# A hybrid mLSTM and pooling layer on eight cores: first-tile loading, engine of the square sums, store times, schedule weights and the place of the final norm changed together

## Chip, cores and metric

The kernel is one layer with an mLSTM (a recurrent layer whose state is a matrix). It runs on all 8 cores of one Trainium2 chip, one sequence per core with no exchange between them. The metric is device microseconds of the slowest core. A program on all cores has two states here: in some executions the cores of one die show a lower granted TensorE clock (down to 0.81 of full, against 0.993 to 0.998), and the time is some per cent longer. Such executions are called slow, whatever the kernel, and are left out of every comparison. Where few executions were fast, I also compare the mean span of single cores on undisturbed dies (all four cores of the die at a clock of 0.992 or more). This "mean core" is below the time of the slowest core but scatters less: for the changed kernel the means of its 20 undisturbed dies lie between 5299.5 and 5306.8 us. The kernel before has mean cores of 5400.3, 5401.0 and 5401.1 us in the calls on three chips, and of 5404.8 in the one profiled execution of the first call. The changed kernel's own call names no chip, so a mean core that differs from it by up to about 4 us is not read as an effect. Where a single step is compared, I also give its mean over the eight cores of each profiled execution, cut at the same count of matmuls on every core (of weight loads, where a trace misses matmul records).

## The reference, cut to what matters

```python
def reference(x, ffn1_..., w_in, b_in, ..., ffn2_..., final_norm_g):      # x (8, 8192, 1024) float32
    x = x + 0.5 * swiglu_ffn(rms_norm(x, ffn1_norm_g), ffn1_w_gu, ffn1_w_down)     # F1, hidden 2816
    x = x + hybrid_mixer(rms_norm(x, mix_norm_g), w_in, ...)                       # the mix
    x = x + 0.5 * swiglu_ffn(rms_norm(x, ffn2_norm_g), ffn2_w_gu, ffn2_w_down)     # F2
    return rms_norm(x, final_norm_g)                                               # final norm
# hybrid_mixer: one projection gives q,k,v,o,u and gates; branch A is an mLSTM over chunks with a norm
# for each head, branch B a trailing mean over 2/4/8/16 tokens; sigmoid gates merge both, one output product
```

## The kernel before

A core takes its sequence in 16 tiles of 512 tokens, kept feature-major (partition, chunk of 128 features, token). A step is a pipeline stage: its main list of units holds F2 of tile i-1 and F1 of tile i+1, its side list the mix of tile i. `interleave` merges both lists into one order by the costs written beside the units. All engines then run that fixed order, each waiting on semaphores for what it reads.

```python
def interleave(main, side, lo, hi):
    ...
            want = lo + (hi - lo) * (ds / tside)      # ds: cost of the side units taken so far
            take_main = dm / tm < want                # dm: cost of the main units taken so far
```

Weights stand in memory as 53 pieces in float32. The first uses of a piece load it with a cast to bf16 (issued by GpSimd); at one use the bf16 copy is stored to scratch, and later uses load that copy (issued by SyncE). A slot that is being stored from is given back one piece later. Six slots hold pieces.

```python
            def store_at(k):                       # at which use of piece k its bf16 copy is stored
                if k < P_F1 + 11:
                    return 0
                if P_QK <= k < P_F2:
                    return k % 2
                return 1
            ...
            def load(tok, s):
                ...
                cast = n <= store_at(k)            # so a late store means one more cast load
```

The norms need a sum of squares over features. ScalarE squares one chunk, GpSimd adds it to the others, and one product with a matrix of ones sums over partitions; then Ln and Exp on ScalarE give the factor.

```python
            def sq(k, x, a):
                ...
                act(sqt[:, k % 2, :], x[:, k, :], AF.Square)
                o = accb[a] if k == KC - 1 else acc[a]
                tt(o[:, :], acc[a][:, :], sqt[:, k % 2, :], ALU.add, eng="pool")

            def norm_rs(a, r, s):
                b = bank(s)                        # main and side have four PSUM banks each, in turn
                mm(PS(b), onesb, accb[a][:, :], True, True)
                act(rs[r][:, :], PS(b), AF.Ln, bias=EPS, scale=1.0 / D)
                act(rs[r][:, :], rs[r][:, :], AF.Exp, scale=-0.5)

            def with_final(main, i):               # final norm and output of tile i, inside F1 of a later tile
                add = final_units(i)               # norm_rs, then four times two products and a store
                ...
                for q, p in enumerate(add):
                    main.insert(4 + 2 * q, p)      # after the fourth product of F1's gate and up list
```

In the mix, the head norm of branch A (Ln and Exp over `sm`) is followed by four units that transpose and gate the result, and by the merge products that read it (`ys`).

```python
                for h in range(H):
                    def run(h=h):
                        ...                        # four transposes on TensorE
                        stt(yaT[:, h, :], PSB(b, 0, 512), pcol(HNG + h), sig[:, h, :], ALU.mult, ALU.mult)
                    us.append((0.5, run))          # the scheduling cost
```

The softmax here doesn't subtract the row's maximum and nothing guards it: scores larger than these inputs give would overflow.

## Time and profile before

| | before |
|---|---|
| median of the first 4 runs | 5425.17 us (5409.37 to 6419.6, the highest a slow one) |
| span of the cores, profiled run | 5396.8 to 5413.9 us, clock 0.993 to 0.994 |
| mean core, undisturbed dies of all calls | 5401.1 us (108 cores) |
| TensorE busy | 97 % of the span |
| one steady step (12 of them) | 330.0 us |
| idle time per steady step that the trace lists | 4.13 us |

TensorE has the work, so the profile is read for TensorE's waits. The waits view adds up the gaps over a stretch by what ended them (columns: engine, tile and line that waited, what came last, us in total, times, longest). For the twelve steady steps, 1096 to 5056 us, of the kernel before:

```profile
PE ps L349 <- DVE ys L377: 23.2, 12, 1.9
PE ps L349 <- ACT tF L370: 12.0, 12, 1.0
PE ps L349 <- POOL accb L373: 8.6, 12, 0.7
PE ps L349 <- DVE hid L373: 5.8, 12, 0.5
```

`ps` is a PSUM bank, to which products write their sums; `xnF` and `xnM` are the normed inputs of the two feed-forward parts and of the mix, `hid` the hidden features, `tF` the result of a Silu, `ys` branch A's result and `accb` the sum of squares. Each gap is small and comes exactly 12 times: 49.6 us in all. The same view of 230 to 1065 us, the early steps, on the slowest core:

```profile
PE ps L349 <- DMA w<-scr: 16.4, 2, 15.1
PE ps L349 <- DMA w<-wsrc: 10.7, 6, 3.0
```

`w<-wsrc` is a cast load, `w<-scr` a load of the stored copy. One row of the page's groups is the exchanges of ScalarE's activation table (columns: line, engine, operation, count, busy us, mean ns, idle before):

```profile
L370 ACT ACT_TABLE_LOAD x221 | 283.5, 1283 | 135.6 <-PE ps L349 113.5
```

### The profile page before, as it was taken

How to read it: one execution, taken by the hardware profiler on the slowest of the kernel's cores; microseconds unless marked ns; L12 is line 12 of the kernel's file. 1: busy time of each engine (PE TensorE's matmuls, PEld its weight loads, DVE VectorE, ACT ScalarE, POOL GpSimd, SP SyncE). 2: the span in 40 equal slices, each digit the busy share in tenths (PEclk: the TensorE clock that was granted, in tenths of full speed). 3: DMA queues.
4: the chain of work that ended last, by engine and by line, in shares of the span. 5: the costliest groups of instructions: out<-in, count | busy, mean ns of one | idle time of the engine just before them, and what ended most of it. 6: DMA issues, size and time to landing. Idle time of an engine off the chain costs nothing.

```text
span 5413.9 us, 74501 instructions; the slowest of 8 cores (5396.8 to 5413.9 us)
## 1 busy us (share of the span) xinstructions
PE 5231.0 (97%) x25247; PEld 2424.5 (45%) x25758; DVE 2074.2 (38%) x3032; ACT 1688.9 (31%) x2973; POOL 1013.1 (19%) x995
## 2 busy tenths in 40 slices
PE   7999989999999999999999999999999999999998
PEld 3444434444444444444444444444444444444443
DVE  2253444244442434434334342443424444343432
ACT  2132333233332323323233232333323333232321
POOL 0121233021121202212022130211212012120310
PEclk9999999999999999999999999999999999999999
DMA  9778799545444344444444444454443444434443
GB/s 221 138 179 173 152 216 237 172 152 179 156 162 166 139 172 159 168 159 143 169 156 170 150 150 170 152 180 152 152 175 137 177 154 173 158 140 159 147 146 121
DMA packets 144130, 883.36 MB, mean 163 GB/s; under 512 B 16144, under 2 KB 18832, under 8 KB 80016
## 3 DMA queue, kind: packets, MB, share of 16 engines
q1 hardware_dynamic: 130368, 800.65, 42.3%
q0 software_dynamic: 12672, 77.08, 9.3%
q8 instruction: 215, 3.52, 0.3%
q14 instruction: 155, 1.27, 0.1%
q10 hardware_dynamic: 720, 0.84, 0.1%
HBM read 873.78 MB, written 81.79 MB: 177 GB/s over the span
## 4 chain that ended last, share of the span: by engine, by line
PE 84%; DVE 5%; ACT 3%; issue 3%; DMA 3%; POOL 1%; DVEq 0%; ACTq 0%; SPq 0%; POOLq 0%
PE ps L349 84%; DVE xnF L377 3%; ACT L370 2%; DMA w<-wsrc 1%; DVE x L377 1%; ACT rs L370 1%; DMA w<-scr 1%; DMA scr<-w 1%; PE ps L353 0%; DVE xnM L377 0%; POOL accb L373 0%; POOL acc L373 0%; ACT sqt L370 0%; ACT tM L370 0%; DVE Cf L373 0%
## 5 line engine op out<-in xcount | busy, mean ns | idle before, releaser
L349 PE MATMUL ps<-xnF,w 128*128 128x512 bf16 x10700 | 2491.8, 380 | 44.3 <-ACT tF L370 13.4
L349 PEld LDWEIGHTS ps<-xnF,w 128*128 128x128 bf16 x10912 | 1063.8, 98 | 1315.9 <-issue 68.0
L349 PE MATMUL ps<-hid,w 128*128 128x512 bf16 x5329 | 1222.2, 380 | 12.5 <-DMA w<-wsrc 5.9
L349 PE MATMUL ps<-xnM,w 128*128 128x512 bf16 x4360 | 1044.8, 380 | 38.1 <-DVE ys L377 24.4
L373 DVE TENSOR_TENSOR hid<-tF,ps 128x512 bf16<-128x512 f32 x682 | 466.5, 686 | 1590.8 <-PE ps L349 1409.0
L373 POOL TENSOR_TENSOR acc<-acc,sqt 128x512 f32<-128x512 f32 x372 | 488.2, 1316 | 2609.3 <-ACT sqt L370 2601.8
L370 ACT ACTIVATE tF<-ps 128x512 f32<-128x512 f32 x704 | 418.6, 597 | 1283.4 <-PE ps L349 1228.9
L349 PEld LDWEIGHTS ps<-hid,w 128*128 128x128 bf16 x5456 | 529.7, 98 | 624.7 <-issue 14.4
L349 PEld LDWEIGHTS ps<-xnM,w 128*128 128x128 bf16 x4448 | 434.7, 98 | 557.7 <-issue 43.9
L377 DVE SCALAR_TENSOR_TENSOR x<-ps,x 128x512 f32<-128x512 f32 x384 | 264.7, 689 | 705.8 <-PE ps L349 658.6
L370 ACT ACTIVATE sqt<-x 128x512 f32<-128x512 f32 x434 | 265.4, 625 | 727.8 <-DVE x L377 577.3
L370 ACT ACTIVATE tM<-ps,pvh 128x512 f32<-128x512 f32 x320 | 219.8, 687 | 785.6 <-PE ps L349 778.8
L377 DVE SCALAR_TENSOR_TENSOR tM<-zy,pv_s,tM 128x512 f32<-128x512 bf16 x384 | 295.2, 771 | 198.1 <-POOL tM L385 159.8
L370 ACT ACT_TABLE_LOAD x221 | 283.5, 1283 | 135.6 <-PE ps L349 113.5
L377 DVE SCALAR_TENSOR_TENSOR tB<-tM,ps 128x512 bf16<-128x512 f32 x256 | 175.8, 687 | 244.6 <-PE ps L349 240.3
L349 PE MATMUL ps<-qkT,w 128*128 128x512 bf16 x1060 | 252.0, 379 | 0.9
L377 DVE SCALAR_TENSOR_TENSOR xnF<-x,pv_s,rs 128x512 bf16<-128x512 f32 x248 | 206.5, 899 | 113.5 <-ACT rs L370 113.4
L385 POOL TENSOR_SCALAR tM<-zy,pv_s 128x512 f32<-128x512 bf16 x128 | 92.9, 729 | 640.4 <-ACT zy L370 585.8
L349 PEld LDWEIGHTS ps<-qkT,w 128*128 128x128 bf16 x1088 | 106.5, 98 | 128.4
L370 ACT ACTIVATE zy<-ps,pv_s 128x512 bf16<-128x512 f32 x128 | 87.5, 684 | 203.0 <-PE ps L349 200.3
L349 PE MATMUL ps<-poolT,w 128*128 128x512 bf16 x530 | 136.6, 379 | 0.7
L349 PE MATMUL ps<-ys,w 128*128 128x512 bf16 x528 | 136.5, 379 | 0.8
(94 smaller groups left out, 2298.8 us busy)
## 6 DMA issues: line engine op xcount, KB each, us to landing
w<-scr SPq DMA_DIRECT2D x409, 1024.0 KB, 5.1
w<-scr SPq DMA_DIRECT2D x224, 704.0 KB, 4.2
w<-scr SPq DMA_DIRECT2D x116, 768.0 KB, 4.4
w<-wsrc POOLq DMA_DIRECT2D x44, 1024.0 KB, 18.2
out<-x SPq DMA_DIRECT2D x64, 512.0 KB, 3.8
x<-x SPq DMA_DIRECT2D x15, 2048.0 KB, 12.2
scr<-w SPq DMA_DIRECT2D x29, 1024.0 KB, 20.0
w<-wsrc POOLq DMA_DIRECT2D x32, 704.0 KB, 15.0
```

Source lines behind the costliest of these rows:

```text
L349: P.op("pe", lambda e: e.matmul(out, lhsT, rhs, start=start, stop=stop), reads=[lhsT, rhs], writes=[out])
L370: P.op("act", lambda e: e.activation(out, in_, func, **kw), reads=rd, writes=wr)
L373: P.op(eng, lambda e: e.tensor_tensor(out, in0, in1, op), reads=[in0, in1], writes=[out])
L377: P.op("dve", lambda e: e.scalar_tensor_tensor(out, in0, scalar, in1, op0, op1), reads=rd, writes=[out])
L385: P.op(eng, lambda e: e.tensor_scalar(out, in0, s1, s2, op0, op1), reads=rd, writes=[out])
```

## The change

The change aims at idle time of TensorE and removes none of its work. It slices the first weight piece and reorders that piece's columns so that a slice serves a whole product; it holds tile 1 back until tile 0 is there; it moves the square additions of steps 0 to 2 and one per step later from GpSimd to VectorE; it stores half of the F1 and F2 down pieces, and half of F2's gate and up pieces, one use later; it stretches the scheduling costs of three mixes by 1.7; it moves the final norm from unit 4 to unit 14; it raises the scheduling cost of the last transposing unit from 0.5 to 1.5; and it gives the last tile a shorter end. It also takes the pooled product first in the merge, lets the mixes of steps 1 and 2 end a little earlier (upper limit 0.92 instead of 0.95), and moves four scalings of a constant (`pb`) in step 0 together. The diff, cut to its core:

```diff
@@ store_at
-                return 1
+                if k < P_QK:
+                    return 1 + k % 2
+                return 1 if k < P_QK or k % 2 else 2
@@ squares
-            def sq(k, x, a):
+            sq_eng = ["dve"]                       # set to "pool" from step 3 on
+            def sq(k, x, a, eng=None):
...
-                tt(o[:, :], acc[a][:, :], sqt[:, k % 2, :], ALU.add, eng="pool")
+                tt(o[:, :], acc[a][:, :], sqt[:, k % 2, :], ALU.add, eng=eng or sq_eng[0])
@@ start
-            load_x(1)
...
-            pieces.prime([0])
+            for q in range(4):
+                c0 = q * 1024
+                dma("pool", P.dma_chan(f"w0_{q}"), wS[0][:, c0:c0 + 1024], wsrc_d[P_F1][:, c0:c0 + 1024], ...)
+            dma("sp", ch_x[1], xb[1][:, :, :], x_d[1], reads=[x0[:, 6:8, :]], writes=[xb[1][:, :, :]])
@@ gate and up products: new column order of a piece
-                        c0 = (256 if up else 0) + jj * 128
+                        c0 = (2 * jj + up) * 1024
@@ down_units: last square of F1 on VectorE; the last tile squares and scales chunk by chunk
+                if sqs == i:
+                    us.append((0.0, lambda: sq(KC - 1, xb[sqs % XB], 0, "dve" if which == "F1" else None)))
+                if last:
+                    us.insert(0, (0.0, lambda: act(sm[:, 11, 0:1], sm[:, 8, 0:1], AF.Ln)))
+                    us.append((0.0, lambda: square_sum(KC - 1)))
@@ mix_units(i, a, lat=1.0): waiting units cost lat times as much; lat is 1.7 in steps 1, 2 and 15
-                @u(6.0)
+                @u(7.0 * lat if i < 3 or lat > 1 else 6.0)
...
-                    us.append((0.5, run))
+                    us.append((0.5 if h < H - 1 else 1.5, run))
...
-                        for wh, src in ((0, yaT), (1, poolT)):
+                        for wh, src in ((1, poolT), (0, yaT)):
@@ with_final
-                    main.insert(4 + 2 * q, p)
+                    main.insert(14 + 2 * q, p)
@@ end
-            for _, p in final_units(nt - 1):
-                p()
+            act(rs[0][:, :], PS(4), AF.Ln, bias=EPS, scale=1.0 / D)
+            act(rs[0][:, :], rs[0][:, :], AF.Exp, scale=-0.5)
+            ...                                    # eight products with rs and four stores
```

## The prediction

> **What bounds the kernel now.** I read the cores view first: all eight span 5396.8 to 5413.9 us at a clock of 0.993 to 0.994, so the profiled run is a fast one. Then the page, for the busiest engine:
>
> ```profile
> span 5413.9 us, 74501 instructions; the slowest of 8 cores (5396.8 to 5413.9 us)
> PE 5231.0 (97%) x25247; PEld 2424.5 (45%) x25758; DVE 2074.2 (38%) x3032; ACT 1688.9 (31%) x2973; POOL 1013.1 (19%) x995
> ```
>
> TensorE has the work, and the change removes none of it. Only its idle time (183 us) and its slow-clock time can go. The windows view, cut at the steps of the program (columns: stretch, length, busy time with counts for PE, PEld, DVE, ACT, POOL, then clock, DMA share, GB/s), shows where these lie:
>
> ```profile
> 24.00:240.00 216.00, 204.96 (x881) 89.88 (x900) 50.58 (x77) 42.54 (x68) 18.37 (x27) 0.98 0.84 172
> 240.00:511.00 271.00, 255.45 (x1236) 117.98 (x1260) 110.45 (x160) 80.43 (x150) 65.07 (x71) 0.97 0.82 179
> 511.00:736.00 225.00, 214.46 (x1060) 99.91 (x1079) 97.63 (x144) 75.76 (x141) 58.12 (x69) 0.98 0.85 165
> 736.00:1096.00 360.00, 331.28 (x1578) 152.26 (x1610) 142.69 (x202) 112.68 (x195) 79.07 (x79) 0.96 0.80 214
> 1096.00:1426.00 330.00, 324.18 (x1578) 150.91 (x1608) 128.45 (x189) 105.84 (x186) 61.03 (x57) 1.00 0.45 160
> 5056.00:5279.00 223.00, 214.56 (x1060) 100.16 (x1078) 90.76 (x137) 75.75 (x141) 45.10 (x44) 0.98 0.40 140
> 5398.00:5414.00 16.00, 0.38 (x1) 0.10 (x1) 6.40 (x9) 3.14 (x4) 1.26 (x1) 0.63 0.32 131
> ```
>
> Step 3 (736 to 1096) holds the same 1578 matmuls as a steady step and takes 360 us, not 330; steady steps (12 of them, 1096 to 5056) hold a full clock. Last, the timeline of TensorE, whose brackets give each gap and what ended it. One steady step has four gaps:
>
> ```profile
> 1430.40 0.38 PE L349 MATMUL ps<-accb,cbf 128*128 128x512 bf16 x1 [0.72 <-POOL accb L373]
> 1589.40 1.89 PE L349 MATMUL ps<-xnF,w 128*128 128x512 bf16 x8 [0.48 <-DVE hid L373]
> 1592.28 5.34 PE L349 MATMUL ps<-xnF,w 128*128 128x512 bf16 x23 [1.00 <-ACT tF L370]
> 1602.17 1.89 PE L349 MATMUL ps<-xnM,w 128*128 128x512 bf16 x7 [1.94 <-DVE ys L377]
> ```
>
> Step 3 has the largest gap of the run, and the end has another:
>
> ```profile
> 817.35 3.57 PE L349 MATMUL ps<-w,xnM 128*128 128x512 bf16 x8 [15.14 <-DMA w<-scr]
> 5401.00 0.38 PE L349 MATMUL ps<-accb,cbf 128*128 128x512 bf16 x1 [3.41 <-POOL accb L373]
> ```
>
> **What the skill says.** (1) "TensorE: Matmul & The Clock Gate", section "Wait — 56ns, not 53.3ns?": matmuls of 512 columns start 215.7 ns apart when warm and 426.7 ns when cold. The trace agrees: 8 take 1.73 us here, and after the 15.14 us gap 8 take 3.57 us. So an idle stretch costs more than its gap. (2) "ScalarE: Activation LUTs", section "What ACT_TABLE_LOAD costs": 1283 ns plus a drain of 1380 ns per switch. The page's row has 1283 ns for one of 221 loads; no such drain shows, for at 1592.15 a load starts 0.01 us after an activation ends and the next starts at 1593.45. (3) "SBUF — State Buffer", section "SBUF: two separate sides": VectorE and GpSimd take one port pair as an exclusive lock for a whole instruction when VectorE has two SBUF inputs. Agreed: eight norm products take 5.39 us with POOL idle and 8.42 us (at 247.76) or 10.44 us (at 731.70) with POOL adding squares. (4) "DMA: Bandwidth & Descriptors", section "Queues, rings and completion order": each DMA engine alternates between queues packet by packet. This fits the start, where x0's third quarter lands at 17.12, just after the first weight piece (its store is issued at 16.93), although quarters one and two landed at 6.8 and 9.2.
>
> **The change, part by part.**
>
> Start. The first weight piece comes in four slices of shorter rows, and x1 waits for x0. x1 stood behind x0 in the same queue, so its delay frees little; what helps is that x0's last two quarters meet shorter weight packets. From 9.2 us, 1 MB of x0 and as much weight at about 250 GB/s take 8 us: x0 complete at some 17 us instead of 19.9. The chain behind it (norm, first matmul at 24.15) is unchanged: 3 us. Risk: weights 2 to 6 are now issued after x1 (near 30 us, before 21.7); the first is needed near 51 us and a 2 MB cast load took about 8 us (5.04 MB bf16 in 40 us), so this is hidden.
>
> Step 0. Four scalings of pb ran just ahead of their matmuls and made two gaps of 1.6 us (85.66, 96.12). They move together to an earlier point: 3 us. They wait for pb, itself now held until weight 2 has landed: about 53 us against 58, so hidden.
>
> Steps 0 to 2: squares move from POOL to VectorE. This frees the port and the POOL queue, which also issues the cast loads (three are issued together at 277.99, behind additions). Step 1 takes 270 us for about 250 of work: 704 main matmuls at 0.216 plus a mix of 98 (the 326 us of a gapless steady step less 228 for 1056 matmuls). Its gaps are norm 0.81 + 1.27, xnM into the gate products 3.5, loads 1.58 + 2.98 + 2.67 + 1.25, and slow clock after them 5: 19. I leave 1.3 for xnM (a chain of 8.5 us behind 33 matmuls of 7.1 us) and 2 for loads: 16 gained. Step 2: norm gaps of 3.5 and the last 0.77 go, 3.3 for xnM, 2 of clock and 1.5 of the mix stay: 5.5 gained.
>
> Step 3. Casting and storing twice overload the DMA. Using 8 us per cast, about 3.5 per 1 MB store or scratch load (5.1 to landing) and 16 for x and out, the first half asks 11 x 11.5 + 5 x 3.5 + 16 = 160 us of 115 us of matmuls. With stores of the even pieces one use later it asks 138, and the buffers had already absorbed about 25 of the old excess of 45. So nearly all of 15.14 + 0.41 + 2.78 goes with 4 us of slow clock; I leave 3. The head (0.26 + 0.98 + 1.29 + 1.08 from the port, 1.40 + 2.31 from three norms exchanging activation tables, 2.5 clock, 1.2 at ys) is some 11 us; 3 stays because eight square additions queue on VectorE. Sum: 22.3 + 11 less 6, call it 26 for rounding and for deferred stores in step 4.
>
> Steady steps. The final norm moves from unit 4 to unit 14. At unit 4 it takes a PSUM bank (the 0.48), meets the head norm's table loads (1258.42, 1260.25, 1262.16) and puts 6.5 us of products before the ys products (the 1.94). Without it the sixth unit takes its bank from a finished product, and only about 0.2 us of the 1.00 stays (silu ready at 1262.15 against 1262.0). Pooled-branch products ahead of ys help too. The last square addition of F1 goes to VectorE, 0.7 instead of 1.27 us, starting earlier: 0.72 becomes about 0.1. Gain 4.13 - 0.3 = 3.8, times 12: 45.5.
>
> Step 15 and end. Cost factors of 1.7 spread the mix: of 2.73 + 0.98 + 0.78 and the clock 4.5 is gained. At the end the last matmul falls at 5397.6 and the end 16.3 later. The new tail is product and square 1.6, matmul 0.5, Ln and Exp 1.3 without a table load, eight products 5, DMA 3.8: 12.3. Seven more sum matmuls cost 1.5: net 2.5.
>
> Sum: 3 + 3 + 16 + 5.5 + 26 + 45.5 + 4.5 + 2.5 = 106 us.
>
> **The rivals.** (a) New waits at the new place: the norm moved to unit 14 meets tanh gates, and its two table switches hold ScalarE for 3.8 us. For it: 221 loads already. Against: four banks for each stream, some 10 us of TensorE work. If it costs 2 us a step, 24 of the 45 vanish: 5340. (b) The DMA stays the bound early: even F2 pieces are cast three times, so step 4 has 6 casts more, and loads queue behind the x load as at 787.18 to 817. For: a DMA share of 0.80 to 0.85 over steps 0 to 3. Against: step 4 asks about 122 us in 115, with full buffers. Cost 10 to 20 us: 5330. (c) Early stages clear entirely, as a change tuned on a chip would: 5 to 10 us more, near 5305. (d) VectorE becomes the bound: 38% busy makes this unlikely.
>
> **Range and chances.** The three fast runs before are 5409, 5415 and 5435, mean 5420. From 106 I take 6 for waits that I can't see, and start from 5418, between this mean and their median: 5318 us. 2% faster needs under about 5311, so the threshold lies inside the error of the step-3 and step-1 terms. Range 5296 to 5344; faster 0.40, within 0.59, slower 0.01.
>
> **What would show it.** Steady steps of 326 us with no gap at ys; step 3 near 334 and step 1 near 254; first weight matmul near 21; last matmul to end near 12. A steady step still at 329 or a load gap above 8 us between 240 and 1400 would make it wrong.

## The result, and the profile after

The changed kernel is correct and takes 5314.74 us (median of 11 runs, 5308.09 to 6310.66). The kernel before took 5415.46 us beside it (median of 17, 5409.37 to 6419.6). The ratio is 0.9821, with a 95 % interval of 0.9795 to 0.9847: 1.8 % faster, with the 2 % line inside the interval. A ratio here is the mean time of one kernel's fast runs over that of the other's in the same rounds, so it is not quite the ratio of these medians. The mean core went from 5401.1 to 5302.6 us (80 cores), 98.5 us less; for the changed kernel the means of its 20 undisturbed dies lie between 5299.5 and 5306.8 us.

The page's first lines of the changed kernel, and its table loads:

```profile
span 5310.7 us, 74865 instructions; the slowest of 8 cores (5293.8 to 5310.7 us)
PE 5241.4 (99%) x25765; PEld 2423.7 (46%) x25765; DVE 2099.5 (40%) x3095; ACT 1659.7 (31%) x2950; POOL 936.1 (18%) x951
L370 ACT ACT_TABLE_LOAD x197 | 252.8, 1283 | 126.5 <-PE ps L349 100.2
```

TensorE is at 99 %, and there are 24 table loads fewer, two for each steady step. (The trace of before misses some 2 % of the matmul records: it has 25247, beside 25758 weight loads. So its PE busy time is not compared.) The windows view, cut at the steps, has the columns of the prediction's windows: stretch, length, busy time with counts for PE, PEld, DVE, ACT, POOL, then clock, DMA share, GB/s. Steps 1, 2 and 3 of the changed kernel:

```profile
234.85:497.47 262.62, 252.73 (x1256) 117.23 (x1255) 121.95 (x188) 80.50 (x150) 39.63 (x54) 0.98 0.82 180
497.47:716.61 219.14, 213.96 (x1079) 99.71 (x1078) 101.60 (x154) 75.71 (x141) 39.79 (x56) 0.99 0.88 175
716.61:1058.99 342.38, 330.44 (x1610) 151.55 (x1609) 141.61 (x206) 112.34 (x196) 69.17 (x72) 0.99 0.73 196
```

Measured from the first matmul of a step to the first of the next, on the profiled (slowest) core of each kernel:

| stretch | before | after | gained | predicted | gained, mean of 8 cores |
|---|---|---|---|---|---|
| start | 24.15 | 21.36 | 2.8 | 3 | 2.6 |
| step 0 | 217.08 | 213.49 | 3.6 | 3 | 3.8 |
| step 1 | 270.14 | 262.62 | 7.5 | 16 | 8.5 |
| step 2 | 224.64 | 219.14 | 5.5 | 5.5 | 6.0 |
| step 3 | 360.07 | 342.38 | 17.7 | 26 | 18.7 |
| 12 steady steps | 3959.9 | 3905.2 | 54.7 | 45.5 | 54.7 |
| step 15 | 222.89 | 214.40 | 8.5 | 4.5 | 7.9 |
| last step and end | 135.07 | 132.13 | 2.9 | 2.5 | 1.4 |
| sum | 5413.9 | 5310.7 | 103.2 | 106 | 103.6 |

The waits of the twelve steady steps of the changed kernel, in the form shown for before:

```profile
PE ps L349 <- DVE accb L373: 0.7, 2, 0.4
```

Three of the four rows are gone and 8.6 us of the fourth have become 0.7. The early steps kept waits for weights, but other ones. First the slowest core, then another core of the same execution, 230 to 1065 us:

```profile
PE ps L349 <- DMA w<-wsrc: 7.4, 1, 7.4
PE ps L349 <- DMA w<-scr: 5.3, 1, 5.3
```

```profile
PE ps L349 <- DMA w<-wsrc: 1.1, 2, 0.8
PE ps L349 <- DMA w<-scr: 0.2, 1, 0.2
```

The program is the same on both; only the transfers fall differently. The eight cores lose 5.6, 12.7, 7.9, 2.0, 8.3, 3.7, 8.0 and 1.3 us in this way, where they lost 14.9 to 27.1 before, and the core with the most is the slowest. The timeline of TensorE (start, length, engine, line, operation, tiles, size, count; in brackets the gap before and what ended it) places its two waits, and one of the gaps left at the head of step 3:

```profile
454.49 1.01 PE L349 MATMUL ps<-qkT,w 128*128 128x512 bf16 x2 [7.37 <-DMA w<-wsrc]
723.66 8.46 PE L349 MATMUL ps<-xnF,w 128*128 128x512 bf16 x32 [1.80 <-DVE x L377]
820.43 1.01 PE L349 MATMUL ps<-xnM,w 128*128 128x512 bf16 x2 [5.26 <-DMA w<-scr]
```

The wait at 454 is new, and all eight cores have it (0.8 to 7.4 us). The product that waits is the first of the mix's output (`qkT`). Its weight piece is cast at its first use in both kernels; what is new are the third cast loads of F1's down pieces, which before were read from scratch by then. With them in the queue, cast loads of 1 MB take 23.6 us to land between 400 and 470 us (median of two on this core), where the kernel before took 13.6 between 405 and 475 (also of two). At the end there is no table load, and the eight products take 6.26 us:

```profile
5299.98 0.60 ACT L370 ACTIVATE rs<-ps 128x512 f32<-128x512 f32 x1 [0.62 <-PE ps L349]
5301.40 6.26 DVE L373 TENSOR_TENSOR x<-x,rs 128x512 f32<-128x512 f32 x8 [2.92 <-ACT rs L370]
```

From the last down product (ended 5297.7) to the end it is 13.0 us, against 16.3 before.

### The profile page after: what moved, and what is told of

Read it like the earlier page. It is cut to its first block, busy times and chain, and to the rows that moved or that the text cites. A ratio compares the mean times of both kernels' runs of the same rounds, so it can differ in the third digit from the quotient of the medians.

```text
span 5310.7 us, 74865 instructions; the slowest of 8 cores (5293.8 to 5310.7 us)
## 1 busy us (share of the span) xinstructions
PE 5241.4 (99%) x25765; PEld 2423.7 (46%) x25765; DVE 2099.5 (40%) x3095; ACT 1659.7 (31%) x2950; POOL 936.1 (18%) x951
## 3 DMA queue, kind: packets, MB, share of 16 engines
q0 software_dynamic: 15120, 89.14, 10.6%
## 4 chain that ended last, share of the span: by engine, by line
PE 94%; DVE 2%; DMA 2%; ACT 1%; issue 1%; POOL 0%; SPq 0%; DVEq 0%; ACTq 0%; POOLq 0%
PE ps L349 93%; DVE tM L377 1%; DMA scr<-w 1%; DVE xnF L377 1%; PE ps L353 1%; DMA w<-wsrc 0%; DMA w<-scr 0%; ACT L370 0%; DVE xnM L377 0%; ACT rs L370 0%; DMA x<-x 0%; DVE x L377 0%; POOL tM L385 0%; DVE x L373 0%; DVE hid L373 0%
## 5 line engine op out<-in xcount | busy, mean ns | idle before, releaser
L349 PE MATMUL ps<-xnF,w 128*128 128x512 bf16 x10912 | 2494.8, 380 | 10.6 <-DVE xnF L377 4.6
L373 POOL TENSOR_TENSOR acc<-acc,sqt 128x512 f32<-128x512 f32 x324 | 424.8, 1315 | 2368.9 <-ACT sqt L370 2296.7
L370 ACT ACT_TABLE_LOAD x197 | 252.8, 1283 | 126.5 <-PE ps L349 100.2
L377 DVE SCALAR_TENSOR_TENSOR xnF<-x,pv_s,rs 128x512 bf16<-128x512 f32 x248 | 184.8, 810 | 99.1 <-ACT rs L370 99.1
L397 POOL DMA_DIRECT2D w<-wsrc x105 | 57.2, 546 | 571.7 <-PE ps L349 442.7
```

The source lines that it names most:

```text
L349: P.op("pe", lambda e: e.matmul(out, lhsT, rhs, start=start, stop=stop), reads=[lhsT, rhs], writes=[out])
L370: P.op("act", lambda e: e.activation(out, in_, func, **kw), reads=rd, writes=wr)
L373: P.op(eng, lambda e: e.tensor_tensor(out, in0, in1, op), reads=[in0, in1], writes=[out])
L377: P.op("dve", lambda e: e.scalar_tensor_tensor(out, in0, scalar, in1, op0, op1), reads=rd, writes=[out])
L397: P.op(eng, lambda e: e.dma_start(out=out, in_=in_), reads=list(reads), writes=list(writes), chan=chan)
```

## The experiments

Twelve kernels ran. All were correct. Most take the changed kernel and undo one part; two put one part alone on the kernel before. Times are of fast runs; "mean core" is as defined above.

| kernel | fast runs, us | mean core (cores) | steady 12 steps |
|---|---|---|---|
| before | 5407.7 to 5435, one 5465.1 | 5401.1 (108) | 3959.9 |
| changed | 5308.1 to 5316.7, one 5365.7 | 5302.6 (80) | 3905.2 |
| 1 norm back at unit 4 | 5310.3, 5310.6, 5312.9 | 5304.5 (32) | not cut |
| 2 norm at 14 alone | 5367.2, 5393.5 | 5359.5 (24) | 3916.7 |
| 3 norm at 4 and old cost | 5361.2 | 5354.1 (12) | 3954.3 |
| 4 new cost alone | 5361.9, 5364.4, 5366.4 | 5354.7 (32) | 3914.7 |
| 5 all stores as before | 5328.0, 5330.2, 5330.6 | 5322.3 (32) | 3905.2 |
| 6 F1 stores as before | 5312.7, 5313.0, 5317.0 | 5306.0 (24) | not cut |
| 7 squares on GpSimd | 5316.0 | 5306.4 (12) | not cut |
| 8 no stretch | 5328.2, 5328.7, 5331.4 | 5320.5 (28) | 3904.6 |
| 9 whole first piece, old end | 5315.3 | 5305.7 (8) | not cut |
| 10 tile 1 not held back | 5309.3 | 5298.8 (12) | not cut |
| 11 attempt | 5307.9 to 5311.8, five | 5302.0 (44) | not cut |
| 12 attempt, fewer deferred | 5307.5, 5308.2 | 5302.6 (32) | not cut |

### 1. The final norm back at unit 4

```diff
-                    main.insert(14 + 2 * q, p)
+                    main.insert(4 + 2 * q, p)
```

> The changed kernel with only the place of the final norm undone (unit 4 again instead of 14). Theory A, the place of the norm is what removed the gaps of 0.48, 1.00 and 1.94 us: each of the 12 steady steps grows from 325.4 to about 328.8 us and the kernel from 5315 to about 5355. Rival B, the 1.94 us went because of the unit of other work after the last transpose and because the pooled products now come first: the steps grow only by 1.5 us (0.48 and 1.00), the kernel to about 5333. Rival C, the gaps went because of something else (squares on VectorE): below 5322.

Measured: 5310.28, 5310.64 and 5312.93 us; ratio to before 0.982 (0.9798 to 0.9842), the same as the changed kernel's. The place of the final norm can be undone at no cost, so undoing it does not bring back the gaps that the prediction put down to it. The timeline of ScalarE near the beginning of an F1 list shows what the prediction missed:

```profile
1212.13 0.52 ACT L370 ACTIVATE sm<-sm 128x16 f32<-128x16 f32 x2 [2.37 <-DVE sm L377]
1213.19 1.28 ACT L370 ACT_TABLE_LOAD   x1
1214.48 1.08 ACT L370 ACTIVATE tF<-ps 128x512 f32<-128x512 f32 x2
1216.19 1.28 ACT L370 ACT_TABLE_LOAD   x1 [0.63 <-PE ps L349]
1217.49 0.60 ACT L370 ACTIVATE rs<-ps 128x512 f32<-128x512 f32 x1
```

The head norm's Ln and Exp (`sm`) run before the first Silu (`tF`) of the list, while the table for Ln and Exp is still in place. In the kernel before they stood behind that Silu and cost a table load on each side. Something else in the change had moved them: a theory for the next runs.

### 2. The final norm at unit 14, alone

```diff
 (kernel before)
-                    main.insert(4 + 2 * q, p)
+                    main.insert(14 + 2 * q, p)
```

> The kernel before with only the place of the final norm changed (14 instead of 4). Theory A: steady steps fall from 330.0 to about 326.6 us (the 0.72 us at the mix norm stays) and the kernel from 5414 to about 5373. Rival B: to 328.5 us and about 5396. Rival C: above 5405. If A holds both here and in the run that undoes it, the place of the norm is worth some 40 of the 103 us on its own.

Measured: one undisturbed run of 5367.23 us, and 5393.45; ratio 0.9948 (0.989 to 1.0005), too few fast runs to say much. The mean core settles it: 5359.5, that is 41.6 us less than before. In the steady steps the waits view has one row left:

```profile
PE ps L349 <- POOL accb L373: 8.6, 12, 0.7
```

(This trace is of the 5393.45 us execution, whose slowest core ran below full clock early on; in these steady steps its clock was 1.00.) So alone, the move does what the prediction said of it. Undone, it costs nothing. Both can be true only if another part does the same. The page still counts all the table loads of the kernel before:

```profile
L370 ACT ACT_TABLE_LOAD x221 | 283.5, 1283 | 135.6 <-PE ps L349 115.3
```

Here the head norm still stands between two Silus, with a load on each side (1279.59 and 1281.42), and only the final norm has gone, to 1306.04. The waits of TensorE vanished without one table load fewer: what counts is which work stands in the queue together, not the number of loads.

### 3. Unit 4 and the old scheduling cost

```diff
-                    us.append((0.5 if h < H - 1 else 1.5, run))
+                    us.append((0.5, run))
...
-                    main.insert(14 + 2 * q, p)
+                    main.insert(4 + 2 * q, p)
```

> The changed kernel with the final norm at unit 4 and the last transpose at its old scheduling weight of 0.5 (the pooled products still first). Undoing the place alone cost nothing, doing it alone gained 3.6 us a step. Theory, the weight of 1.5 shifts the head norm's Ln and Exp ahead of the first Silu, so that either measure suffices: with both undone the gaps come back, the steady step is 328.5 to 329.5 us and the kernel near 5355. Rival, the order of the products is what makes the place harmless: the step stays at 325.5 and the kernel near 5315.

Measured: 5361.16 us; mean core 5354.1, 51.5 us more than the changed kernel. The twelve steps take 3954.3 us, 49.1 more, and the three old rows are back in the waits of this stretch:

```profile
PE ps L349 <- DVE ys L377: 23.6, 12, 2.3
PE ps L349 <- ACT tF L370: 12.0, 12, 1.0
PE ps L349 <- DVE hid L373: 5.8, 12, 0.5
```

ScalarE in one of these steps:

```profile
1876.26 0.60 ACT L370 ACTIVATE tF<-ps 128x512 f32<-128x512 f32 x1
1876.88 1.28 ACT L370 ACT_TABLE_LOAD   x1
1878.17 0.53 ACT L370 ACTIVATE sm<-sm 128x16 f32<-128x16 f32 x2
1878.71 1.28 ACT L370 ACT_TABLE_LOAD   x1
1880.01 0.60 ACT L370 ACTIVATE tF<-ps 128x512 f32<-128x512 f32 x1
1880.62 1.28 ACT L370 ACT_TABLE_LOAD   x1
1881.92 0.60 ACT L370 ACTIVATE rs<-ps 128x512 f32<-128x512 f32 x1
```

Silu, load, head norm, load, Silu, load, final norm: ScalarE exchanges its table for every small piece of work, and in the same stretch TensorE waits 0.48 us (for a bank, by the prediction's reading), 1.00 us for a Silu and 1.9 us for `ys`. Again 221 table loads. Together, runs 1 and 3 show that the place can be undone as long as the cost stays. That each part suffices alone, run 2 shows for the place and run 4 for the cost. The pooled product comes first in this run too, and the wait for `ys` is back in full (23.6 us, 23.2 before): that order alone does not remove it.

### 4. The new scheduling cost, alone

```diff
 (kernel before)
-                    us.append((0.5, run))
+                    us.append((0.5 if h < H - 1 else 1.5, run))
```

> The kernel before with one edit: the scheduling cost of the last of the four transposes-and-gate products of ya is 1.5 instead of 0.5, and the final norm stays at unit 4. If this weight is enough by itself, as the run with the place undone and the run with place and weight undone say together, a steady step takes about 326.4 us, the gap of 1.94 us at the ya products is gone, and the kernel takes about 5370 us (5360 to 5385). Rival: the weight only counts together with the other parts of the change (squares, order of the gate products); then a steady step stays at 329 to 330 us and the kernel at 5400 to 5415 us.

Measured: 5361.89, 5364.40 and 5366.44 us. The ratio of 0.9867 (0.9744 to 0.9989) rests on two fast runs of before, one of them at 5465; the mean core of 5354.7 is 46.4 us below before. The twelve steps take 3914.7 us (326.2 each), with these waits:

```profile
PE ps L349 <- POOL accb L373: 8.6, 12, 0.7
PE ps L349 <- DVE hid L373: 0.6, 1, 0.6
```

One number in a scheduling list, with no instruction added or removed, is worth nearly half of the whole change. How it works can be read from `interleave`: a larger cost at the end of the side list raises its total, so every earlier side unit is taken a little sooner, and the products after the raised unit a little later. By the costs in the list, one unit more moves the order by about 228 x 0.95 / 146 = 1.5 us of main products (an estimate from these costs). That is enough to put the head norm ahead of the first Silu (in this trace `sm` starts at 1247.02, the table load at 1248.08 and the Silu at 1249.37), and the wait for `ys` is gone. Table loads fall to 195. What is left, 0.7 us a step, is the wait for the last square addition on GpSimd, which the change moves to VectorE: 3914.7 - 3905.2 = 9.5 us for twelve steps, of which 8.6 are this wait.

### 5. All stores as before

```diff
-                if k < P_QK:
-                    return 1 + k % 2
-                return 1 if k < P_QK or k % 2 else 2
+                return 1
```

> The changed kernel with the old store times (no piece is cast a third time). Theory, spreading the stores removed the 15 us wait for a scratch load in step 3: that wait comes back at 10 to 15 us on the cores, with waits for cast loads in step 3 of 2 to 4 us; step 3 grows from 342 to about 358 us, the kernel to about 5330. The late wait of 7.4 us near 454 us goes. Rival, what removed it is the POOL queue, freed of squares so that casts are issued in time: step 3 stays within 3 us of 342 and the kernel within 4 us of 5315.

Measured: 5327.99, 5330.17 and 5330.6 us, ratio to before 0.9854 (0.9831 to 0.9876) where the changed kernel has 0.9821; mean core 19.7 us above the changed kernel. Step 3 takes 355.5 us in place of 342.4. The cores wait 16 to 27 us for weights between 230 and 1065 us, as they did before the change. One of them:

```profile
PE ps L349 <- DMA w<-wsrc: 15.3, 7, 2.9
PE ps L349 <- DMA w<-scr: 7.7, 1, 7.7
```

The deferred stores carry about 20 us, and most of it in step 3: 13.1 us on the slowest cores, 17.7 in the mean of eight. This is the prediction's reason, and it holds in the main. The expectation missed the form: not one scratch wait of 10 to 15 us came back (the longest is 7.7), but several waits of up to 2.9 us for cast loads, 15.3 us on this core.

### 6. Only the stores of F1 as before

```diff
-                    return 1 + k % 2
+                    return 1
```

> The changed kernel with the old store times for the F1 down pieces alone (cast twice, stored on the second use); F2 keeps the change. Theory, the third cast of the odd F1 pieces made the new wait near 454 us (1 to 7 us by core), and the old waits of 3 to 9 us near 290 to 315 us come back in its place, as when both halves were undone: the sum of load waits between 230 and 1065 us, 1.3 to 12.7 us by core in the changed kernel, stays within 4 us and so does the time (5315). Rival, the F1 half only adds casts: the wait near 454 goes and nothing comes back, 5306 to 5310. Second rival, the F1 half carries the gain: load waits of 15 us and more, 5325 or above.

Measured: 5312.69, 5313.03 and 5316.99 us. Against the changed kernel's 5314.74 this is no difference, and the mean core's 3.4 us is within the 4 us of scatter. The new wait at 454 is gone, but two others stand in its place:

```profile
286.23 2.53 PE L349 MATMUL ps<-hid,w 128*128 128x512 bf16 x11 [2.03 <-DMA w<-wsrc]
303.62 1.86 PE L349 MATMUL ps<-hid,w 128*128 128x512 bf16 x4 [7.26 <-DMA w<-wsrc]
```

Storing F1's pieces early makes the loads of step 1 late near 286 and 303 us; storing them late makes a load late at 454 us. The wait is moved and, in these two executions, grows: the cores' waits for weights between 230 and 1065 us are 10.1 us in the mean here, 6.2 in the changed kernel. So the F1 half is worth 4 us at most, and by subtraction the F2 half carries most of the gain of run 5; it was not undone alone.

### 7. The squares of steps 0 to 2 back on GpSimd

```diff
-            sq_eng = ["dve"]
+            sq_eng = ["pool"]
```

> The changed kernel with the squares of steps 0 to 2 on POOL again (the last addition of each F1 pass stays on VectorE). Theory, they held the shared port and the POOL queue: in step 1 the eight xnM products take over 8 us again instead of 5.4 and the gates' wait for xnM grows from 0.9 to about 3.5 us, cast loads are issued late again, and step 3's head stalls 3 to 4 us on xnF; together 8 to 15 us, about 5327. Rival, moving them to VectorE only exchanged one wait for another (8 additions queue before xnM in step 3): within 4 us of 5315.

Measured: one fast run, 5315.98 us; mean core 5306.4, 3.8 us above the changed kernel, which is within the 4 us of scatter. The trace of the slowest core shows waits exchanged for others:

```profile
487.69 0.38 PE L349 MATMUL ps<-accb,cbf 128*128 128x512 bf16 x1 [1.28 <-POOL accb L373]
721.73 1.02 PE L349 MATMUL ps<-xnF,w 128*128 128x512 bf16 x4 [3.06 <-DMA w<-wsrc]
```

These appear, while 1.25 and 1.80 us at the head of step 3, where the additions queue on VectorE, disappear. The second is the slowest core's alone. Averaged over the eight cores, step 1 takes 264.3 us against 258.0 in the changed kernel (258.9 in run 1), and step 3 takes 1.0 less. Of the 6 us in step 1 the waits that the trace lists make about 2.4: 1.3 for `accb` and some 1.1 more for `xnM`; the rest is open. The eight `xnM` products there take 7.41 us beside GpSimd's additions and 5.39 without, less than the expected "over 8", and the products that wait for `xnM` lose 2.5 us and not 3.5. In all the move is worth about 4 us; nothing at all is not excluded by a single fast run.

### 8. The mixes not stretched

```diff
-                 mix_units(0, 0, 1.7)),  ...  mix_units(1, 0, 1.7)),  ...  1.7 if i == nt - 1 else 1.0
+                 mix_units(0, 0)),       ...  mix_units(1, 0)),       ...  1.0
-                @u(7.0 * lat if i < 3 or lat > 1 else 6.0)
+                @u(6.0)
-                    interleave(main, side, 0.0, 0.95 if n > 2 else 0.92)
+                    interleave(main, side, 0.0, 0.95)
```

> The changed kernel with the stretch of the mixer's scheduling costs taken out (factor 1.7 back to 1.0 in steps 1, 2 and 15, the norm's cost back to 6, the upper limit back to 0.95). If the stretch, and not the move of the squares to VectorE, carries the gains of steps 1, 2 and 15, these steps grow by about 5, 3 and 5 us and the kernel takes 5323 to 5330 us. Rival: the squares and the stores carry them; then the kernel stays within 4 us of the changed kernel, 5311 to 5318 us.

Measured: 5328.17, 5328.65 and 5331.43 us; mean core 5320.5, 17.9 us above the changed kernel. The windows of step 3 and step 15 of this kernel:

```profile
720.48:1066.18 345.70, 330.76 (x1611) 152.23 (x1610) 144.31 (x209) 110.03 (x194) 69.34 (x72) 0.98 0.70 191
4970.74:5194.33 223.59, 215.42 (x1080) 99.89 (x1079) 92.11 (x140) 75.98 (x141) 43.94 (x43) 0.98 0.39 139
```

On this core step 15 takes 8.0 us more than in the changed kernel cut in the same way (215.6), step 1 takes 3.0 more (265.65) and step 3 takes 3.3 more; step 2 does not change (219.0). In the mean of eight cores the steps 1, 2, 3 and 15 grow by 3.4, 0.3, 7.4 and 7.0 us. The total is as expected, the parts are not: 5, 3 and 5 were expected of steps 1, 2 and 15, and nothing of step 3. There, two waits stand on this core:

```profile
728.79 0.53 PE L349 MATMUL ps<-accb,cbf 128*128 128x512 bf16 x1 [4.92 <-DVE accb L373]
825.83 1.44 PE L349 MATMUL ps<-xnM,w 128*128 128x512 bf16 x3 [8.00 <-DMA w<-scr]
```

Step 3's own mix is not stretched in either kernel, though the cost of its norm goes from 7 back to 6. A reading of the first wait is that step 2's mix now ends later (the upper limit is 0.95 again), so that tile 2's additions are late for step 3's first norm. The second was 5.26 us in the changed kernel. Over all cores the waits for weights between 230 and 1065 us rise from 6.2 to 15.4 us in the mean, nearly all of it in loads of the stored copy (2.2 to 10.6). So part of what the stretch gains is that weights come in time; the expectation did not name this, and no run shows how. For step 15 a reading is that a stretched mix gives each link of a dependent chain more main products to lie behind, where the main list is short; it was not tested apart from the rest.

### 9. The first piece in one transfer, and the old end

```diff
-            for q in range(4): ...                 # four slices of the first piece
+            dma("pool", P.dma_chan("w0_0"), wS[0][:, :], wsrc_d[P_F1], writes=[wS[0][:, :]])
...                                                 # and the end of the kernel before
```

> The changed kernel with two far-apart parts undone at once, each read from its own end of the trace: the first weight piece comes as one load (x1 still held until x0 is in), and the last tile has the old end. Theory for the start, weight packets with long rows take turns with those of x0: x0's last quarter lands near 19.9 us again and the first weight matmul is at 23.5 to 24.5 us. Rival, holding x1 is what moved it: last quarter near 17 us, first weight matmul near 21.4. For the end: from the last product of the down matmuls to the end 16.3 us instead of 13.1 or so, with an activation-table load of 1.3 us in the chain and a wait of 3.4 us for POOL's sum.

Measured: 5315.26 us, one look. The first weight product and the last eight products:

```profile
22.95 1.25 PE L349 MATMUL ps<-xnF,w 128*128 128x512 bf16 x2 [2.48 <-DVE xnF L377]
5301.14 1.28 ACT L370 ACT_TABLE_LOAD   x1 [2.24 <-PE ps L349]
5303.86 6.75 DVE L377 SCALAR_TENSOR_TENSOR x<-x,pv_s,rs 128x512 f32<-128x512 f32 x8 [5.79 <-ACT rs L370]
```

The start is at 22.95, between the changed kernel (21.36) and before (24.15), and below the expected 23.5: the slices give about 1.6 us of the 2.8 (1.3 of 2.6 in the mean of eight cores). What gives the other 1.2 is open; tile 1 is still held back in this run, which with the piece in one transfer may matter. The end takes 16.7 us from the last down product in place of 13.0, so the new end is worth 3.7 us, less the seven more sum products; the whole last step is 2.2 us longer here in the mean of cores.

### 10. Tile 1 not held back

```diff
+            load_x(1)                              # again right behind tile 0, in the same queue
...
-            dma("sp", ch_x[1], xb[1][:, :, :], x_d[1], reads=[x0[:, 6:8, :]], writes=[xb[1][:, :, :]])
```

> The changed kernel with x1 issued right behind x0 as before, the first weight piece still in four slices. Theory (packets of the weight slices): x0's last quarter still near 17 us and the first weight matmul near 21.4 us, x1 lands earlier. Rival (x1 competes with x0): last quarter near 19.5 us or later.

Measured: 5309.3 us, one look.

```profile
21.17 3.23 PE L349 MATMUL ps<-xnF,w 128*128 128x512 bf16 x5 [2.50 <-DVE xnF L377]
```

The first weight product starts at 21.17 us, as in the changed kernel. With the slices in place, holding tile 1 back changes nothing at the start. The mean core of 5298.8 us is 3.8 lower, on three dies of one chip, within the 4 us of scatter; so whether tile 1 is better not held back stays open.

### 11 and 12. Attempts at something faster

Three gaps of the changed kernel looked removable: 1.32 + 3.76 us in step 0 (the first norm of tile 1, done in one block), and the head of step 3, where eight square additions wait on VectorE.

```diff
 (changed kernel)
-                    us[:8] = [us[n] for n in (0, 2, 4, 6)] + [(0.0, lambda: first_norm(1, xnM, hid, 1))] + [us[n] for n in (1, 3, 5, 7)]
+                    us[:8] = ([us[n] for n in (0, 2)] + [(0.0, lambda: first_squares(1, hid))] + [us[4]]
+                              + [(0.0, lambda: first_rest(1, xnM, hid, 1))] + [us[n] for n in (6, 1, 3, 5, 7)])
-            squares2 = [(0.5, lambda k=k: sq(k, xb[2], 1)) for k in range(KC)]
+            squares2 = [(0.5, lambda k=k: sq(k, xb[2], 1, "pool")) for k in range(KC)]
-                us.append((2.0 * lat, lambda: None))
+                us.append((5.0 if i == 2 else 2.0 * lat, lambda: None))
...                                                 # and tile 1 not held back, as in run 10
```

> An attempt to improve on the changed kernel: the squares of tile 1 are taken as soon as it lands and its norm ahead of the fourth product of the first weight piece, tile 1 is not held back, the eight square additions of tile 2 go to GpSimd, and the mixer of step 3 starts some 3 us later in the order. If the gaps that the trace of the changed kernel lists are independent, 1.3 + 2.5 us are gained in step 0 and 3 of the 6.2 us at the head of step 3: about 5307 to 5309 us, 0.12 % faster. Rival: the loads of weights set the end of the early steps and give the gain back as longer waits for loads; then 5312 to 5316 us.

Measured: 5307.9, 5309.02, 5309.4, 5310.71 and 5311.78 us. The slowest core is some 3 us better than the changed kernel's fast runs, but the mean core is 5302.0, against 5302.6: no gain that can be shown. Step 0 did become 3.7 us shorter (210.1), and step 3 became 2.0 longer (344.4), for this at its head:

```profile
716.47 0.38 PE L349 MATMUL ps<-xnF,w 128*128 128x512 bf16 x1 [1.29 <-DVE xnF L377]
718.14 1.71 PE L349 MATMUL ps<-xnF,w 128*128 128x512 bf16 x4 [1.30 <-DVE xnF L377]
```

With the additions on GpSimd, VectorE's norm products (`xnF`) come late again, 1.3 us each time, as at this place in the kernel before, where both engines also worked side by side.

The second attempt also defers only two of the eight down pieces of F1 instead of four:

```diff
-                    return 1 + k % 2
+                    return 2 if k % 4 == 3 else 1
```

> The attempt before with two instead of four of the down pieces of F1 stored one use later. If the waits near 303 us (all stored early, 7.3 us) and near 454 us (four stored late, 7.4 us) are two ends of one trade, with two both become about 3 us or less and one of them the rest, and the kernel gains another 2 to 5 us: 5303 to 5307 us. Rival: either wait comes back at nearly full size, because the queue is short by more than one piece at both places; then no gain over the attempt before, 5307 to 5314 us.

Measured: 5307.52 and 5308.16 us, the other four runs slow. The waits of the slowest core, 230 to 1065 us:

```profile
PE ps L349 <- DMA w<-wsrc: 3.4, 1, 3.4
```

The longest single wait for weights is 3.5 us on any core, near 294; the mix's first output product no longer waits. Summed over a core, these waits are 3.1 us on average (4.9 at most) where the changed kernel has 6.2. The mean core is 5302.6 us, unchanged; only the spread shrinks (the standard deviation of a core's span is 3.9 us, against 6.3). As the slowest core sets the time, this may be worth 3 to 5 us, but two fast runs don't show it. I call neither attempt faster than the changed kernel.

## Why the prediction was right or wrong

**The total** was right: 5318 predicted, 5314.7 measured, and the change by sum 103.2 us against 106. The prediction held "within 2 %" for a little likelier than faster (0.59 to 0.40) and put the 2 % line inside its error; the interval measured does contain that line. The terms were not all right: steps 1 and 3 came out 17 us too high together, the steady steps and step 15 13 us too low. That these errors cancelled is luck, so the total is no proof of the parts. Of the signs named in advance, the steady step (325.4 us, no gap at `ys`) and the first weight product (21.4) came; the end (13.0, not 12), step 3 (342.4, not 334) and step 1 (262.6, not 254) fell short. Neither sign of being wrong came, the load gap by little: 7.37 us against its limit of 8.

**Steady steps: size nearly right, cause half right.** Predicted 3.8 us each, measured 4.56. The gaps that the trace listed sum to 4.13, and nearly all went. The rest lies in gaps that are not listed one by one: with the same three gaps back (run 3) the stretch grows by 49.1 us for 41.4 us of listed waits. The prediction put the gain on the move from unit 4 to unit 14. Run 2 shows that this move alone does it; run 1 shows that it can be undone. The step that failed is one that is missing: the prediction didn't mention the scheduling cost raised from 0.5 to 1.5, which by itself gives 46.4 us (run 4). It also gave the order of the merge products a share, and run 3 shows none. Rival (a), new waits at unit 14, did not happen: 0.7 us in twelve steps.

**Step 1: 16 predicted, 7.5 measured.** The prediction listed 19 us of waits and slow clock and left 2 for loads. In its place a load wait of 7.37 us stands at 454, the eight products after it take 3.57 us instead of 1.89, and a new wait of 1.57 us (for `tM`) stands at 293. The load wait is rival (b), cast loads that the change itself adds, though the prediction looked for them in step 4. Run 6 shows that it belongs to F1's deferred stores, and that without them waits of the same kind stand at 286 and 303. The prediction's other reason for step 1, squares on VectorE, holds: undone, step 1 grows by some 6 us (run 7). The stretched mix, to which it gave nothing here, gives 3 (run 8).

**Step 3: 26 predicted, 17.7 measured.** The mechanism holds in the main: the 15.14 us wait went, and undoing the stores returns 13.1 us in this step, 17.7 in the mean of cores (run 5). It is not alone: undoing the stretch returns 7.4 us in the mean (run 8), a share that the prediction did not see, and the two together exceed the 18.7 gained, so they overlap. The term "I leave 3" for loads was mis-sized: 5.26 us remained at 820 on the slowest core. So was "3 stays" for the head, where the four larger gaps sum to 6.2 us. The prediction read one core; load waits differ from 1.3 to 12.7 us between cores of one execution, and the slowest core is by choice the one with the most.

**Step 2** gained 5.5 as predicted, but no run shows by what: undoing stores, squares or stretch changes it by 0.8, 0.5 and 0.3 us in the mean of cores. **Step 15: 4.5 predicted, 8.5 measured**; the cause named, the stretched costs, is right, and its removal costs 8.0 (run 8). The prediction counted 4.5 us of gaps; the timeline before lists 7.4 in this step, of which 2.5 remain, and the mean clock of the step went from 0.98 to 1.00.

**Start and end: sizes right.** 2.8 for 3, and 2.9 for 2.5. At the start the prediction chose the slices over the delay of tile 1 as what helps; run 10 agrees, and by run 9 the slices give a little over half. Its rate of 250 GB/s stands in no trace: from 9.2 to 20 us the kernel before moved 232. At the end the eight products take 6.26 us, not 5, and the whole tail 13.0, not 12.3.

**The sum by undoing**, in mean core: place and cost 51.5, stores 19.7, stretch 17.9, squares 3.8, slices and end 3.1, together 96.0 of 98.5 us. With up to 4 us of scatter in each term, so close a sum is partly chance. Each was undone by itself except the two pairs. Undone one by one, place and cost would have counted for nothing, and the sum would have been short by half: run 1 shows it for the place, and for the cost it is inferred from run 2. The scalings of pb in step 0, the order of the two merge products and the last square of F1 were not tried alone; the 9.5 us of run 4's remainder is an argument for the last of them, and run 3, where it stays on VectorE and the wait for `accb` stays away, is another.

## What to carry to other kernels

A part that costs nothing when undone may still be the cause, if another part does the same work; try each part alone on the kernel before as well, and both undone together. In a kernel whose engines run a fixed order, the numbers that make the order are part of the change: read them in the diff as carefully as a new instruction, and look on ScalarE's timeline for what stands in front of the work that TensorE waits for. The count of table loads does not price it: run 2 removed the waits with all 221 loads in place. A wait for loads that is removed in one place while the transfers stay as many tends to come back at another, and it should be read on all cores: the slowest sets the time, but its trace alone put 3.3 us on a step where the mean of cores had 7.4 (run 8).

## What the Trainium skill lacked or had wrong

- "ScalarE: Activation LUTs", section "What ACT_TABLE_LOAD costs": it gives 1283 ns for the load and about 1380 ns more for a drain with every switch. The load's 1283 ns is what every page here shows (195 to 221 loads). The drain is not: in run 3 a Silu ends at 1876.86, the load starts at 1876.88, and the next activation starts at 1878.17, so the switch took 1.31 us. An estimate by the page's figure would have priced the 24 loads removed at 64 us; at 1.28 each they are 31 us of ScalarE's time, and what they cost TensorE is neither: in run 2 its waits went with no load fewer.
- "TensorE: Matmul & The Clock Gate", section "Seeing it yourself": it says that a die goes to 13/16 of the clock once three of its cores run dense matmuls, and to budget for that. In the fast executions here all eight cores ran dense bf16 matmuls (PE busy 99 %) at a mean granted clock of 0.993 to 0.998. Lower means, from 0.81, came in 52 of the 92 executions whose cores are listed, in 40 of them on one die only. Nor need it hold a whole die or last: in the profiled execution of run 2, cores 6 and 7 had a clock of 0.81 from 320 to 480 us and of 1.00 in the steady steps, while cores 4 and 5 of the same die had 1.00 in both. What starts it no run here shows.
- No page that I read has it that waits for weights differ so much between cores that run the same program: 1.3 to 12.7 us in one execution of the changed kernel, 14.9 to 27.1 before. A single core's trace does not size them.
